# Tree attention on one core: three stores and two layings moved in GpSimd's program, and Q of heads 16 to 31 loaded in rows of sixteen nodes

## The chip, the cores and the metric

The kernel runs on one core of a Trainium2 chip. The core has a matrix engine (TensorE, called PE in the profile, with PEld for its weight loads), a vector engine (VectorE, DVE), a scalar engine (ScalarE, ACT), a general engine (GpSimd, POOL) and sixteen DMA engines that serve queues filled by POOL, SP and ACT. The metric is the device time of one execution in microseconds; the median over several runs is given. Before the change it is 132.79 us (3 runs, 132.54 to 132.94).

## The reference

Attention over 96 heads (8 x 12), each with 512 nodes of width 64, in float32. The nodes are those of a binary tree in heap order, and a node attends only to itself and its ancestors:

```python
mask = np.zeros((seq, seq))
for i in range(seq):
    mask[i, i] = 1
    parent = i
    while parent > 0:
        parent = (parent - 1) // 2
        mask[i, parent] = 1

scores = np.einsum('bhqd,bhkd->bhqk', Q, K) * scale
scores = scores + (1 - mask) * (-1e9)
weights = np.exp(scores - np.max(scores, axis=-1, keepdims=True))
weights = weights / (np.sum(weights, axis=-1, keepdims=True) + 1e-10)
return np.einsum('bhqk,bhkd->bhqd', weights, V).astype(np.float32)
```

Q, K and V have 12.6 MB each, and so has the output.

## The kernel before

**Pairs, quads and blocks.** The kernel works on pairs of heads, 48 of them, numbered i. For each pair it forms scores in two parts (`scores1`: the upper nodes as keys, `scores2`: each query's own tile of leaves), with the mask added as a product of codes on TensorE, takes exponentials on ScalarE (two instructions for the first part's 1024 columns and the second part's halves), multiplies by V with a column of ones (`values`), and divides on VectorE (`norm`: a reciprocal of the column of sums and a product). `head(i, a)` tells which two heads a pair has. Loads come in blocks: K and Q in blocks of 8 heads (`KB`), V in blocks of 16 (`VB`). The block number of V is called o below.

**Three forms of Q and K.** A load casts float32 to bf16 and lays nodes on partitions. In the narrow form (pairs below `WIDE` = 8, heads 0 to 15) a partition holds 4 nodes of one head, in rows of 512 bytes of bf16. In the wide form two heads share the partitions and a row has 8 nodes (1024 bytes); in the far form four heads share them and a row has 16 nodes (2048 bytes). Q is far from pair `FAR` = 16 on (head 32), K from pair `KFAR` = 24 on (head 48). `turn` transposes K or Q of a pair (narrow) or of two pairs (wide and far) on TensorE into `ktp` or `qtp`, and VectorE copies them to where the matmuls read them. The far form of Q is turned in two halves of a quad of pairs; `far_q` hands on the queries of all four pairs (`qTs`) only when its second half has been copied. From pair `FAR` on a pair of a quad has heads 8j + r and 8j + r + 4.

**V.** It lands in a staging tile, `vst`, of which there are three. From block 1 on its rows come in parts: "upper" (the first 64 rows), and "even" and "odd" in block 1 or "leaves0" and "leaves1" in later blocks. Copies (`spread`) bring pieces of it to the places of the matmul operand `vt`, of which there are two, on VectorE (table `BY_VECTOR`, then `STEADY_VECTOR`), on ScalarE (`BY_SCALAR`, `STEADY_SCALAR`) and on GpSimd (`spread_top`, `spread_pool`). `far_codes` are four small copies on ScalarE that lay out the mask's codes for the far form of Q; `FAR_CODES` gives the pairs at which they are done.

**What sets the order.** Nothing is scheduled automatically; every engine works in the order in which the program emits instructions for it. The main loop over i follows a string of steps for each pair: S (both scores of pair i), V (values and norm of pair i - 1), K and Q (the next turn), D and A (the table's V copies on VectorE and ScalarE, at the end if the letter is missing), W (a small copy of codes), X (idle matmuls). `FIRST` holds the strings of the first pairs; later ones repeat with period 2 or 4.

**GpSimd's program.** GpSimd issues almost all DMAs: the loads (`load_k`, `load_q`, `load_v`, `load_rows`) and nearly all stores, each of a block of 8 heads, 1024 KB. It also copies V, and for the last two blocks of K and Q (80 to 87 and 88 to 95) it lays heads side by side in another tile (`lay_beside`). All these are entries of one list, `pool_program()`, taken strictly in order; `ready` tells from which pair on an entry may be emitted. A wait of one entry holds back all after it. Before the change the stores are put into the list by a rule: `BEHIND` = 56 heads behind the loads.

Of the kernel before, what the change touches and what calls it, by code (L numbers as in the profile page):

```python
# [13 lines left out]
BEHIND = 56  # L14
# [105 lines left out]
def kernel(  # L120
# [15 lines left out]
    WIDE, FAR, KFAR = 8, 16, 24  # L136
# [622 lines left out]
    def pool_program():  # L759
# [5 lines left out]
            (load_q, 12, 4), (load_k, 16, 4), (load_rows, 1, "upper"),  # L765
            (load_q, 16, 4), (load_rows, 1, "even"), (load_k, 20, 4), (load_rows, 1, "odd"),
            (load_q, 20, 4), (load_k, 24, 8), (load_q, 24, 4), (load_rows, 2, "upper"),
            (load_q, 28, 4), (load_rows, 2, "leaves0", "leaves1"), (load_k, 32, 8), (load_q, 32, 8),
# [7 lines left out]
        loaded, stored = 72, 0  # L776
        for h in range(56, NH, KB):
            top = [(spread_top, h // VB + 0)] if h % VB == 8 and 4 <= h // VB + 0 < NH // VB else []
            if top:
                top.append((spread_pool, (h // VB, "Z0", 0, 16), (h // VB, "Z1", 0, 16)))  # L780
            ops += [(load_k, h, KB)] + top + [(load_q, h, KB)]
            if h == 64:
                ops.append((
                    spread_pool, *[(3, part, 0, 16) for part in ("Z0", "Z1", "X", "M", "D1")]
                ))
            while loaded < min(h + 32, NH):
                names = ("leaves0", "leaves1") if loaded % VB else ("upper",)
                ops.append((load_rows, loaded // VB) + names)
                loaded += KB
            if top:  # L790
                o = h // VB
                ops.append((spread_pool, *[(o, part, 0, 16) for part in ("X", "M", "D1")]))
            if stored + KB + BEHIND <= h + KB:
                ops.append((store, nc.gpsimd, stored, KB))
                stored += KB
        ops.insert(-1, (lay_beside, "kst", 80 // KB))
        while stored < NH - KB:
            n = 2 if stored == APART else 0
            ops.append((store, nc.gpsimd, stored + n, KB - n))
            if stored == 40:  # L800
                ops.append((lay_beside, "qst", 80 // KB))
            if stored == 64:
                ops += [(lay_beside, "kst", 88 // KB), (lay_beside, "qst", 88 // KB)]
# [169 lines left out]
```

## Time and profile before

| | |
|---|---|
| median of 3 runs | 132.79 us |
| profiled execution | 132.49 us |
| its span, first to last instruction | 130.7 us |
| mean granted clock | 0.986 |
| bytes moved, as the DMA packets count them | 32.25 MB |
| HBM read, written | 37.94 MB, 12.58 MB |

The profile is one execution. A timeline row has the start, the busy time, the engine, the line of the kernel, the operation and its tiles; in brackets stands how long the engine was idle before it and what ended that. A row of the windows table has, after the window, for each engine the busy time and the number of instructions, then the granted clock, the mean share of the DMA engines that packets took (above 1 where an engine has several packets under way) and GB/s. A row of the chain of waits has start, length and what the chain passed through. A row of the DMA issues has the number of DMAs, KB of each and the median time from issue to landing.

### The profile page before, as it was taken

The numbers are of one execution on the slowest core, as the hardware profiler recorded it, in microseconds if no ns is written. First come the engines' busy times: TensorE is split into PE (matmuls) and PEld (weight loads), VectorE is DVE, ScalarE is ACT, GpSimd is POOL, SyncE is SP. The second block draws the span as 40 slices with busy tenths as digits, with TensorE's granted clock in tenths as the row PEclk, the third lists the DMA queues.
The fourth block names the chain that finished last, engine by engine and source line by source line (L and its number), as shares of the span: only waits on it lengthen the run. The fifth ranks groups of instructions, "written<-read, shape, count | busy, mean of one in ns | idle before, by whom it ended". The sixth has DMA issues, their size and how long they took to land.

```text
span 130.7 us, 5436 instructions
## 1 busy us (share of the span) xinstructions
PE 113.7 (87%) x2353; PEld 81.0 (62%) x2353; DVE 105.6 (81%) x254; ACT 101.1 (77%) x163; POOL 84.4 (65%) x116
## 2 busy tenths in 40 slices
PE   6688969999799887899998999896999997999940
PEld 2354755766577566677776786674677675776630
DVE  3349779888999998989998998987898997894560
ACT  4179676989779995968987799797689785889930
POOL 6999625354483999995299899953999963202130
PEclk9999999999999999999999999999999999999995
DMA  2999999999999999999999999999999999999984
GB/s 89 248 190 192 201 195 201 201 202 205 201 203 208 208 205 207 208 210 205 207 211 201 283 292 210 270 309 231 338 228 322 257 277 397 402 404 386 382 339 145
DMA packets 26071, 32.25 MB, mean 247 GB/s; under 512 B 1240, under 2 KB 19544, under 8 KB 26048
## 3 DMA queue, kind: packets, MB, share of 16 engines
q0 software_dynamic: 24384, 30.41, 111.4%
q1 hardware_dynamic: 944, 0.91, 2.2%
q10 hardware_dynamic: 720, 0.59, 1.5%
q8 instruction: 18, 0.29, 0.8%
q14 instruction: 5, 0.04, 0.1%
HBM read 37.94 MB, written 12.58 MB: 386 GB/s over the span
## 4 chain that ended last, share of the span: by engine, by line
DVE 29%; DMA 28%; PE 22%; POOL 7%; ACT 6%; issue 4%; ACTq 0%; DVEq 0%; POOLq 0%
DMA vst<-in_V_dram 17%; DMA qst<-in_Q_dram 11%; DVE of L735 9%; PE ob L696 8%; DVE vt L374 6%; PE s L601 3%; DVE qq L577 3%; ACT e L652 3%; DVE rec L733 3%; DVE kk L521 3%; POOL kst L247 2%; PE s L608 2%; DVE kk L525 2%; POOL qst L247 2%; ACT e L618 2%
## 5 line engine op out<-in xcount | busy, mean ns | idle before, releaser
L618 ACT ACTIVATE e<-s 128x1024 bf16<-128x1024 f32 x40 | 40.9, 1024 | 15.0 <-PE s L608 14.6
L696 PE MATMUL ob<-vt,e 128*128 128x65 bf16 (+1 forms) x940 | 37.1, 197 | 2.6 <-DVE of L735 1.0
L696 PEld LDWEIGHTS <-e 128*128 128x128 bf16 (+1 forms) x960 | 30.1, 102 | 9.6 <-DVE of L735 1.9
L374 POOL COPY vt<-vst 32x512 int32<-32x512 int32 (+4 forms) x44 | 32.5, 739 | 4.7 <-PE ob L696 2.5
L652 ACT ACTIVATE e<-s 128x384 bf16<-128x384 f32 x80 | 34.7, 490 | 0.0
L735 DVE TENSOR_TENSOR of<-ob,rec 128x512 f32<-128x512 f32 x47 | 32.5, 691 | 1.6
L374 DVE COPY vt<-vst 32x1024 bf16<-32x1024 bf16 (+5 forms) x47 | 20.9, 445 | 2.8 <-DMA vst<-in_V_dram 1.9
L743 POOL DMA_DIRECT2D out_dram<-of x13 | 11.5, 888 | 12.9 <-DVE of L735 12.4
L733 DVE RECIPROCAL rec<-ob 128x8 f32<-128x8 f32 x47 | 9.5, 202 | 9.9 <-PE ob L696 9.3
L257 POOL DMA_DIRECT2D kst<-in_K_dram x11 | 8.0, 725 | 7.4 <-DMA qst<-in_Q_dram 3.2
L601 PE MATMUL s<-far,codes 40*128 40x512 bf16 x64 | 12.5, 386 | 0.0
L635 PEld LDWEIGHTS <-codes 40*128 40x128 bf16 x80 | 6.2, 94 | 8.7 <-issue 3.9
L614 ACT ACTIVATE e<-s 128x1024 bf16<-128x1024 f32 x8 | 8.2, 1023 | 4.1 <-PE s L608 4.0
L577 DVE COPY qq<-qtp 128x1024 bf16<-128x1024 bf16 x16 | 10.9, 680 | 0.3 <-PE qtp L572 0.3
L635 PE MATMUL s<-far,codes 40*128 40x384 bf16 x64 | 10.7, 324 | 0.4 <-ACT e L652 0.2
L257 POOL DMA_DIRECT2D qst<-in_Q_dram x12 | 8.5, 708 | 3.8 <-DMA vst<-in_V_dram 1.9
L374 ACT COPY vt<-vst 32x512 int32<-32x512 int32 (+3 forms) x19 | 10.4, 545 | 0.4
L608 PE MATMUL s<-qq,kk 64*128 64x512 bf16 x48 | 9.2, 378 | 1.0 <-DVE qq L577 1.0
L646 PEld LDWEIGHTS <-kk 64*128 64x128 bf16 x192 | 8.4, 94 | 2.6
L521 DVE COPY kk<-ktp 128x256 bf16<-128x256 bf16 x24 | 9.0, 414 | 0.7 <-PE ktp L513 0.7
L302 POOL DMA_DIRECT2D vst<-in_V_dram x7 | 5.6, 800 | 6.0 <-DMA vst<-in_V_dram 4.3
L572 PE MATMUL qtp<-ptile,qst 128*64 128x128 bf16 x192 | 7.5, 221 | 1.7 <-DVE qq L577 1.0
(64 smaller groups left out, 178.2 us busy)
## 6 DMA issues: line engine op xcount, KB each, us to landing
out_dram<-of POOLq DMA_DIRECT2D x10, 1024.0 KB, 15.2
kst<-in_K_dram POOLq DMA_DIRECT2D x9, 512.0 KB, 16.5
qst<-in_Q_dram POOLq DMA_DIRECT2D x8, 512.0 KB, 14.8
vst<-in_V_dram POOLq DMA_DIRECT2D x12, 256.0 KB, 13.5
vst<-in_V_dram POOLq DMA_DIRECT2D x6, 512.0 KB, 12.9
qst<-in_Q_dram POOLq DMA_DIRECT2D x6, 256.0 KB, 12.1
kst<-in_K_dram POOLq DMA_DIRECT2D x4, 256.0 KB, 10.3
out_dram<-of POOLq DMA_DIRECT2D x1, 768.0 KB, 13.0
```

Of the source, the lines that this page charges most:

```text
L257: return nc.gpsimd.dma_start(out=kept[b][:, h0 % KB:h0 % KB + n, :, :].rearrange("p (g x) t d -> p g (x t d)", x=x), in_=src[:, h0 // x:(h ...
L374: return copy(out=dst, in_=src)
L521: nc.vector.tensor_copy(out=columns(flat, 32 * unit, (640, 4), (step, 2), (4, 8), (1, 4)), in_=columns(kp, base, (256, 4), (128, 2), (1, 8 ...
L577: nc.vector.tensor_copy(out=qqs[j][:, :, 8 * last:8 * last + 8, :].rearrange("p b u c -> p b (u c)"), in_=quarters,)
L601: nc.tensor.matmul(out=sp[:, a, :], lhsT=(k1code if i < WIDE else k1wide)[64 * a:64 * a + CODE_ROWS, :], rhs=(q1code, q1wide, q1far)[(i >= ...
L608: nc.tensor.matmul(out=sp[:, a, :], lhsT=keys(i, a, TOP), rhs=qTs[i][64 * a:64 * a + 64, :, :].rearrange("p t c -> p (t c)"), start=False, ...
L618: ) if i < WIDE else nc.scalar.activation(
L635: nc.tensor.matmul(out=flat[:, a, :, :].rearrange("p u (t c) -> p u t c", t=4)[:, :, :, 32 // n:], lhsT=k2wide[64 * a:64 * a + CODE_ROWS, ...
L652: nc.scalar.activation(out=e2s[i % NE][:, a, :, 32:128].rearrange("p t (r u) -> p t r u", u=n), in_=flat[:, a, :, :].rearrange("p u (t r) ...
L696: nc.tensor.matmul(out=ob[lo:hi, a, 65 * t:65 * t + 65], lhsT=e[:, a, PLACE[t], lo:hi], rhs=vt[vtile[tile_v][0]][:, head(i, a) % VB, vtile ...
L733: nc.vector.reciprocal(out=rec[:, a:a + n, :, :], in_=o4[:, a:a + n, :, D:D + 1])
L735: nc.vector.tensor_tensor(out=ofs[j][:, h0:h1 + 1:head(i, 1) - head(i, 0), :, :], in0=o4[:, a:a + n, :, 0:D], in1=rec[:, a:a + n, :, :].to ...
```

## The change

GpSimd's list from head 56 on is written out by hand. Against the old order:

- Store of heads 8 to 15 stands behind the loads of K and Q of heads 72 to 79 and the V copies there; store 16 behind K and Q of 80; store 24, with store 32, behind K and Q of 88, the V copies of block 5 and the laying of block 80. (Store 0 keeps its place behind the leaves of V block 4.)
- The upper rows of V block 5 stand behind K and Q of 64, GpSimd's copies of V block 3 and the leaves of block 5, where they stood ahead of store 0 and of K of 64.
- Both layings of block 80 stand ahead of stores 24 and 32, both of block 88 ahead of stores 40 to 64.

For heads 16 to 31, `FAR` becomes 8: the wide form of Q isn't used any more, pairs 8 to 15 take their heads as quads do, and both halves of Q of a quad are turned before its first scores (steps Q at pairs 6 and 7 for pairs 8 to 11, at 10 and 11 for pairs 12 to 15; before at 6, 8, 10 and 12). K and Q of heads 16 to 31 are loaded eight heads at a time, and "upper", "even" and "odd" of V block 1 stand behind Q of heads 16 to 23. The far codes are laid out at pairs 4 to 7 and ScalarE's three first copies of V block 1 are done at pair 8 together.

```diff
-    WIDE, FAR, KFAR = 8, 16, 24
+    WIDE, FAR, KFAR = 8, 8, 24
...
-            (load_q, 12, 4), (load_k, 16, 4), (load_rows, 1, "upper"),
-            (load_q, 16, 4), (load_rows, 1, "even"), (load_k, 20, 4), (load_rows, 1, "odd"),
-            (load_q, 20, 4), (load_k, 24, 8), (load_q, 24, 4), (load_rows, 2, "upper"),
-            (load_q, 28, 4), (load_rows, 2, "leaves0", "leaves1"), (load_k, 32, 8), (load_q, 32, 8),
+            (load_q, 12, 4), (load_k, 16, 8), (load_q, 16, 8),
+            (load_rows, 1, "upper"), (load_rows, 1, "even"), (load_rows, 1, "odd"),
+            (load_k, 24, 8), (load_q, 24, 8), (load_rows, 2, "upper"),
+            (load_rows, 2, "leaves0", "leaves1"), (load_k, 32, 8), (load_q, 32, 8),
...
-            if stored + KB + BEHIND <= h + KB:
-                ops.append((store, nc.gpsimd, stored, KB))
-                stored += KB
-        ops.insert(-1, (lay_beside, "kst", 80 // KB))
-        while stored < NH - KB:
-            n = 2 if stored == APART else 0
-            ops.append((store, nc.gpsimd, stored + n, KB - n))
-            if stored == 40:
-                ops.append((lay_beside, "qst", 80 // KB))
-            if stored == 64:
-                ops += [(lay_beside, "kst", 88 // KB), (lay_beside, "qst", 88 // KB)]
-            stored += KB
+        def tops(o):
+            return [(spread_top, o), (spread_pool, (o, "Z0", 0, 16), (o, "Z1", 0, 16))]
+
+        def rest(o):
+            return [(spread_pool, (o, "X", 0, 16), (o, "M", 0, 16), (o, "D1", 0, 16))]
+
+        def out(h0, n=KB):
+            return [(store, nc.gpsimd, h0, n)]
+
+        def leaves(o):
+            return [(load_rows, o, "leaves0", "leaves1")]
...
+        ops += k7 + q7 + leaves(4) + out(0)
+        ops += k8 + q8 + [(spread_pool, *[(3, part, 0, 16) for part in ("Z0", "Z1", "X", "M", "D1")])]
+        ops += leaves(5) + [(load_rows, 5, "upper")]
+        ops += k9 + tops(4) + q9 + rest(4) + out(8)
+        ops += k10 + q10 + out(16)
+        ops += k11 + tops(5) + q11 + rest(5)
+        ops += [(lay_beside, "kst", 80 // KB), (lay_beside, "qst", 80 // KB)] + out(24) + out(32)
+        ops += [(lay_beside, "kst", 88 // KB), (lay_beside, "qst", 88 // KB)]
+        for h in range(40, NH - KB, KB):
+            n = 2 if h == APART else 0
+            ops += out(h + n, KB - n)
         ops += [(store, nc.gpsimd, NH - KB + h, 2) for h in (0, 4)]
...
-        6: [(1, 6, 0, 8)],
-        7: [(1, "Z0", 0, 8)],
-        8: [(1, "Z1", 0, 8)],
+        8: [(1, 6, 0, 8), (1, "Z0", 0, 8), (1, "Z1", 0, 8)],
...
-    FAR_CODES = {9: (0, 0), 10: (64, 0), 11: (0, 1), 13: (64, 1)}
+    FAR_CODES = {4: (0, 0), 5: (64, 0), 6: (0, 1), 7: (64, 1)}
...
-    FIRST = ['KSQ', 'SXKQXDVAKQ', 'SVKQ', 'SKQAV', 'KSVXQA', 'SAKQVDW', 'SKDVQ', 'SVD', 'SVDKQX']
+    FIRST = [
+        'KSQ', 'SXKQXDVAKQ', 'SVKQ', 'SKQAV', 'KSVXQA', 'SAKQVDW', 'SKDVQ', 'SVQD', 'SVDKX', 'SVK',
+        'SVQ', 'SVKQ', 'SV',
+    ]
...
-        elif i == FAR - 1:
+        elif i == 2 * WIDE - 1:
             steps = "SQVK"
```

More of the change, by code (lines that the diff above doesn't have):

```diff
@@ L775, in pool_program @@
         ]
[L776 to L792, printed above, removed]
-            if stored + KB + BEHIND <= h + KB:
-                ops.append((store, nc.gpsimd, stored, KB))
-                stored += KB
@@ new lines, in rest, with qk @@
+        def rest(o):
[4 more added lines that the diff above has]
+            return [(load_rows, o, "leaves0", "leaves1")]
+        def qk(h0):
+            return [(load_k, h0, KB)], [(load_q, h0, KB)]
+        k7, q7 = qk(56)
+        k8, q8 = qk(64)
+        k9, q9 = qk(72)
+        k10, q10 = qk(80)
+        k11, q11 = qk(88)
+        ops += k7 + q7 + leaves(4) + out(0)
```

1 line of the change is left out of this document (removed).

## The prediction

> **What bounds the kernel now.** I read the page first (busy shares, the DMA row), then a table by windows, then the timelines of the engines round the places that the change touches.
>
> ```profile
> PE 113.7 (87%) x2353; PEld 81.0 (62%) x2353; DVE 105.6 (81%) x254; ACT 101.1 (77%) x163; POOL 84.4 (65%) x116
> DMA  2999999999999999999999999999999999999984
> 10.00:20.00 10.00, 8.39 (x176) 5.56 (x172) 8.17 (x24) 7.58 (x12) 5.88 (x9) 1.00 1.44 196
> 50.00:60.00 10.00, 9.42 (x229) 7.07 (x224) 8.94 (x21) 6.72 (x12) 9.06 (x16) 1.00 1.19 209
> 110.00:120.00 10.00, 9.76 (x189) 7.15 (x187) 8.02 (x18) 8.46 (x16) 0.83 (x1) 1.00 1.03 400
> 125.00:129.50 4.50, 0.75 (x16) 0.52 (x14) 1.76 (x5) 0.18 (x1) 0.45 (x1) 0.74 0.83 291
> 129.50:130.70 1.20, 0.00 (x0) 0.00 (x0) 0.00 (x0) 0.00 (x0) 0.00 (x0) 0.50 0.00 0
> ```
>
> In the window rows the last three numbers are the granted clock, the DMA share and GB/s. The DMA engines are full from the second slice to the last but one: about 200 GB/s while the loads land as bf16 (196 with 512-byte rows, 209 with the longer ones), 400 while only stores run. All bytes of the kernel pass this stream in the order in which POOL issues them, and neither their number nor their end changes by moving a store. The stream has slack only at its end: from 125.0 to 129.5 it is 0.83 busy against 1.03 in the window of stores, so 4.5 x (1 - 0.83/1.03) = 0.9 us is empty. No order of stores can win more than about that, call it 1.0.
>
> But the engines stand close to the stream (PE 8.4 to 9.8 of 10 us). Where a load lands just as it is wanted, its place in the stream sets the pace:
>
> ```profile
> 80.91 0.64 PE L513 MATMUL ktp<-ptile,kst 128*64 128x128 bf16 x16 [0.23 <-DMA kst<-in_K_dram]
> 83.62 0.64 PE L572 MATMUL qtp<-ptile,qst 128*64 128x128 bf16 x16 [0.45 <-DMA qst<-in_Q_dram]
> 91.38 0.64 PE L513 MATMUL ktp<-ptile,kst 128*64 128x128 bf16 x16 [0.98 <-DMA kst<-in_K_dram]
> 93.87 0.64 PE L572 MATMUL qtp<-ptile,qst 128*64 128x128 bf16 x16 [0.23 <-DMA qst<-in_Q_dram]
> 85.92 0.21 DVE L733 RECIPROCAL rec<-ob 128x8 f32<-128x8 f32 x1 [0.42 <-PE ob L696]
> 92.06 0.75 DVE L521 COPY kk<-ktp 128x256 bf16<-128x256 bf16 x2 [0.68 <-PE ktp L513]
> 79.25 14.58 DMA qst<-in_Q_dram
> ```
>
> These are the K and Q blocks of heads 64 to 79: the transposes start at landing, PE loses 0.23 + 0.45 + 0.98 + 0.23 = 1.9 us, and VectorE, which is nearly as full, loses 0.42 + 0.68 = 1.1 us of it. The last row is of the chain of waits, which goes through such a landing.
>
> **Part 1, the stores.** One store, as POOL issues it, and the laying that now stands ahead:
>
> ```profile
> 72.36 0.91 POOL L743 DMA_DIRECT2D out_dram<-of  x1
> out_dram<-of POOLq DMA_DIRECT2D x10, 1024.0 KB, 15.2
> 90.23 4.87 POOL L374 COPY vt<-vst 32x512 int32<-32x512 int32 x6 [2.49 <-PE ob L696]
> 95.05 0.70 POOL L257 DMA_DIRECT2D qst<-in_Q_dram  x1
> 95.79 2.95 POOL L374 COPY vt<-vst 32x1024 int32<-32x1024 int32 x3
> 98.93 1.04 POOL L448 COPY kst<-kst 128x1024 int32<-128x1024 int32 x1 [0.19 <-DMA kst<-in_K_dram]
> 100.49 0.61 PE L507 MATMUL ktp<-ptile,kst 128*128 128x128 bf16 x8
> ```
>
> 1024 KB at 400 GB/s is 2.6 us of the stream. Store 8 goes behind K and Q of heads 72, store 16 behind K and Q of 80, store 24 behind K and Q of 88; so from head 72 on each K and Q block has one store less ahead of it and lands 2.6 us earlier. The upper part of V block 5 goes from ahead of K of head 64 to behind Q and the leaves; it is 512 KB at 209, about 2.5 us, and gives heads 64 to 71 the same lead. 2.6 us is more than any wait above, so all four vanish. POOL's own work is unchanged in number (0.91 us a store, 1.04 a laying). The stream doesn't run dry: loads wait some 14 us between issue and landing, and moving one store takes 2.6 of that.
>
> What the waits return: between 1.1 us (VectorE's loss) and 1.9 us (PE's). I take 1.1, as VectorE comes next, and so does POOL: from the values of pair 31, which release POOL at 90.23, to the end of the laying of K it takes 4.87 + 0.70 + 2.95 + 1.04 = 9.6 us, to 99.8 without its 0.19 of waiting; PE takes that K at 100.49 today. A gain of over 0.7 us between these points ends in a wait for POOL. As lower end I keep 0.5, if both bite. The layings ahead of stores 24 to 64 delay these by up to 10 us; the stream still has stores 24 and 32 (5.2 us) behind Q of head 88, more than the about 2.2 us for two layings and an issue: nothing.
>
> **Part 2, longer rows and larger loads.** Heads 16 to 31 of Q, 1 MB as bf16, go from 1024 to 2048 bytes a row. At the worst rate above, 196, they take 5.35 us, at 209 5.0: the stream wins 0 to 0.35 us. I take 0.15, and count it as nothing, since the end follows the last values. Three loads fewer: 3 x 0.7 us of POOL (the row at 95.05), which isn't the bound there. The Trainium skill, "DMA: Bandwidth & Descriptors", section "Anatomy of one DMA", has a fixed cost of about 2 us for each DMA, besides its bytes; by that, three DMAs fewer would take an estimated 6 us off a queue that ran one at a time. The DMA share of 1.19 to 1.44 in the rows above says that they overlap, and disagrees for this queue.
>
> **Part 3, the front.** Here Q's new form costs: in quads of pairs, both halves of Q must be turned and copied before the quad's first scores.
>
> ```profile
> 18.50 12.18 DMA vst<-in_V_dram
> 25.45 1.02 ACT L614 ACTIVATE e<-s 128x1024 bf16<-128x1024 f32 x1
> 30.75 1.35 DVE L374 COPY vt<-vst 128x1024 bf16<-128x1024 bf16 x3 [0.44 <-DMA vst<-in_V_dram]
> 32.08 0.62 ACT L374 COPY vt<-vst 32x512 int32<-32x512 int32 x1
> 33.09 1.02 DVE L374 COPY vt<-vst 32x1024 bf16<-32x1024 bf16 x3
> 35.14 0.68 DVE L549 COPY qq<-qtp 128x1024 bf16<-128x1024 bf16 x1
> 35.17 0.67 ACT L396 COPY far<-codes 40x512 bf16<-40x512 bf16 x1
> 42.28 0.90 DVE L374 COPY vt<-vst 32x1024 bf16<-32x1024 bf16 x2
> 43.20 0.21 DVE L733 RECIPROCAL rec<-ob 128x8 f32<-128x8 f32 x1
> 44.05 0.68 DVE L549 COPY qq<-qtp 128x1024 bf16<-128x1024 bf16 x1
> 51.68 0.38 PE L608 MATMUL s<-qq,kq 64*128 64x512 bf16 x2
> 52.16 1.02 ACT L618 ACTIVATE e<-s 128x1024 bf16<-128x1024 f32 x1 [1.56 <-PE s L608]
> 52.35 0.79 PE L696 MATMUL ob<-vt,e 128*128 128x65 bf16 x20
> 53.08 0.87 ACT L652 ACTIVATE e<-s 128x384 bf16<-128x384 f32 x2
> ```
>
> VectorE's work there is the same, in another order, so I book what it waits.
> - The "odd" rows of V block 1 land at 18.50 + 12.18 = 30.7, and VectorE waits for them. They now stand behind 256 KB more of Q: 0 to 1.3 us at 200 GB/s, since both loads are in the stream together today. I take +0.55. That wait then covers the copy of Q's second half (0.68, at 35.14 today), due at pair 7 now: -0.7.
> - The code copies (L396, 0.67) go from pairs 9, 10, 11, 13 to 4 to 7; at 4 and 5 nothing leaves in exchange, so the exponentials from 25.45 on come up to 1.3 us later. On VectorE most of it falls into the wait at 30.75: 0.1 (0 to 0.6). After pair 9 ScalarE gets the time back.
> - At pair 8 ScalarE copies three pieces of V in one go, and values(8) need them all. Q's copy ends at 31.3, the exponential starts 0.5 later (51.68 to 52.16), two exponentials 1.8, three pieces 1.9, values 0.8: 36.3. VectorE has the first norm at 32.8 (31.3 and 1.5 through scores and values, 51.68 to 53.14), 0.85 for it (43.20 to 44.05), 1.0 of V, 1.0 of K (34.11 to 35.14): 35.7. It waits 0.6 at most; with copies that overlap a little, 0.4 (0 to 1.0).
> - At pair 12 the scores wait for Q's copy, which VectorE now does behind norm(10) and K; today it runs after norm(11), at 44.05. From there to the end of the values is 1.5 us again, and VectorE has only the 0.90 of row 42.28 meanwhile: it idles 0.6. For norm(12), the exponentials of 12 end 2.3 after the key matmuls (51.68 to 53.95), the second scores of 13 need the buffer then freed (0.4, from 51.68 to 52.35 less the 0.3 that the key matmuls take), the values take 0.79: 3.5. VectorE has by then done 1.5, a norm of 0.85 and a piece of V of 0.45 to 0.9: about 3.0, so 0.5 more. Together 1.1 (0.5 to 2.0; the upper end if ScalarE's 1.56 at 52.16 is lost whole once more).
>
> Sum of the front: 0.55 - 0.7 + 0.1 + 0.4 + 1.1 = +1.45, call it 1.5, with ends 0.5 and 2.5. No load is late between there and 80.91, so nothing gives it back before the waits above.
>
> **POOL in the middle.** The first copies of V block 3 overwrite rows that belong to heads 24 to 27; in the new order of heads these are read up to pair 15, not 13.
>
> ```profile
> 48.65 5.35 POOL L374 COPY vt<-vst 32x1024 int32<-32x1024 int32 x7
> 53.95 0.84 POOL L302 DMA_DIRECT2D vst<-in_V_dram  x1
> 62.88 0.70 POOL L257 DMA_DIRECT2D kst<-in_K_dram  x1 [1.81 <-DMA qst<-in_Q_dram]
> 65.43 0.70 POOL L257 DMA_DIRECT2D qst<-in_Q_dram  x1 [1.85 <-DMA vst<-in_V_dram]
> ```
>
> Values of pair 15 end at 53.14 + 1.5 = 54.6; the last four of the seven copies end at 53.95 today and could only start then, so what is queued behind them (V upper of block 4, K, Q and leaves) is issued some 2.7 us later. POOL waits 1.81 + 1.85 = 3.7 us for landings soon after, which swallows it, and the stream holds 14 us: nothing (0 to 0.5).
>
> **The sum.** +1.5 (front) - 1.1 (waits returned) = +0.4 us at the last values, and the end follows them. The profiled execution is 132.49 us, 130.7 of span and 1.8 around it: 132.9. The median of the runs shown, 132.79, is 0.3 above; on it the forecast is **133.2 us**. With the ends (0.5 to 2.5, less 1.9 to 0.5) it is -1.4 to +2.0, and the stream stops the gain at -1.0: 131.8 to 134.8.
>
> **Rivals.**
> 1. *The earlier loads win* (faster). Price 1.9 us at 80.91 to 93.87, all on PE's path, against a front of 0.5 to 0.9. It decides where the front costs less than what the waits return. For it speaks that PE, not VectorE, is named in all four rows; against it POOL's 9.6 us and that VectorE is 0.9 full in the front. Bounded by the stream: -1.0, 131.8; its middle 132.1. Chance 0.24.
> 2. *It cancels out*, or the end of the stream holds the time: within 0.3, 132.8. For it speaks the full DMA row. Chance 0.14.
> 3. *POOL turns into the bound.* Its late copies at 54.6 aren't swallowed, or the laying of K at 99.8 makes PE wait although the loads are there: the waits return 0.5 or less and the front costs 2: +1.5, 134.3. Chance 0.14.
> 4. *Fewer, larger transfers shorten the stream*: the 1 MB of Q and as much of its neighbours gain all of 196 to 209, 2 x 0.35 = 0.7 at most, middle 0.5: 132.3. The page of the Trainium skill named above points that way with its fixed cost. The rows show a stream that is full without it. Chance 0.03.
>
> **How the numbers follow.** The forecast's own case has 0.45 (132.8 to 133.9): 0.31 of it lies above 133.2, 0.14 below. A measurement here tells about 0.3%, 0.4 us, from no change. Slower: 0.31 + 0.14 = 0.45. Faster: rival 1 with 0.22 and rival 4 with 0.03, 0.25. Same: 0.14 + 0.14 + 0.02 = 0.30. The range 131.8 to 134.5 reaches from the stream's floor to past rival 3.
>
> **What would show it.** Transposes of K and Q of heads 64 to 79 without a DMA as releaser; scores of pair 12 released by VectorE's copy, with ScalarE idle some 2 us ahead of them; the values of pair 15 (52.35) 1 to 2 us later; the laying of K right ahead of its transposes; DMA share over 1.0 until about 120. Wrong it is if these values come at the same time, or if K and Q of heads 64 to 79 are still waited for.

## The result and the profile after

The changed kernel takes 136.17 us (median of 6 runs, 135.21 to 136.82), the kernel before 132.77 us beside it (6 runs, 132.53 to 132.94): 1.0247 times as long, 95% interval 1.0216 to 1.0278. It is slower by 3.4 us, where 0.4 was forecast, and lies outside the range of 131.8 to 134.5. A ratio below leaves out runs over 1.5% longer than the fastest of the same kernel, so it can disagree with a median; where many runs are long, as in e2 and e3, both are needed.

The profiled execution took 136.02 us, with a span of 134.3 us against 130.7. From its page: the busy times, the slices of the granted clock and of the DMA engines, and the issues of whole stores.

```profile
PE 115.0 (86%) x2350; PEld 81.8 (61%) x2353; DVE 108.9 (81%) x254; ACT 100.8 (75%) x163; POOL 82.3 (61%) x113
PEclk9999999999999769999999999999999999999995
DMA  3999999999999999999999999999999899999974
out_dram<-of POOLq DMA_DIRECT2D x10, 1024.0 KB, 11.2
```

There are four things to see. The clock has a dip at slices 14 and 15. The DMA engines, which were full to the last slice but one, have a thin slice at 105 us and a thin end. A store now waits 11.2 us from issue to landing and not 15.2: less is queued ahead of it. VectorE has 3.3 us more of work than before (108.9 against 105.6) with the same 254 instructions.

What the forecast had said of the loads came true. The timeline of PE in the changed kernel at K and Q of heads 64 to 79:

```profile
84.13 0.61 PE L512 MATMUL ktp<-ptile,kst 128*64 128x128 bf16 x16
86.20 0.61 PE L571 MATMUL qtp<-ptile,qst 128*64 128x128 bf16 x16
93.57 0.61 PE L512 MATMUL ktp<-ptile,kst 128*64 128x128 bf16 x16
95.64 0.61 PE L571 MATMUL qtp<-ptile,qst 128*64 128x128 bf16 x16
```

None of them has a bracket any more: PE waits for none of these loads.

The last values end later by 2.7 us. VectorE's division for the last pair, 47, is done head by head; it starts at 125.79 us before and here, in the changed kernel's timeline, at 128.47:

```profile
128.47 0.18 DVE L732 RECIPROCAL rec<-s 128x4 f32<-128x4 f32 x1
```

The rest of the 3.5 us of span, some 0.85 us, arises behind the last values. The windows of the kernel before:

```profile
100.00:105.00 5.00, 4.97 (x105) 3.70 (x102) 4.42 (x11) 4.19 (x8) 5.00 (x6) 1.00 1.10 282
105.00:110.00 5.00, 4.31 (x84) 3.15 (x81) 4.35 (x9) 3.50 (x7) 2.62 (x3) 1.00 1.08 338
110.00:115.00 5.00, 5.00 (x104) 3.92 (x102) 4.01 (x10) 4.28 (x9) 0.83 (x1) 1.00 1.02 398
```

and of the changed one, with two short windows in it:

```profile
100.00:105.00 5.00, 4.72 (x101) 3.33 (x97) 4.87 (x11) 4.07 (x8) 4.82 (x6) 1.00 1.08 213
105.00:110.00 5.00, 4.49 (x91) 3.33 (x87) 4.82 (x11) 3.81 (x7) 4.96 (x7) 1.00 0.94 347
110.00:115.00 5.00, 4.54 (x99) 3.49 (x96) 4.05 (x10) 3.62 (x8) 2.39 (x3) 1.00 0.98 330
104.50:106.00 1.50, 1.50 (x38) 1.22 (x33) 1.49 (x4) 1.50 (x3) 1.50 (x3) 1.00 0.75 176
110.50:112.00 1.50, 1.12 (x19) 0.66 (x15) 1.47 (x4) 0.57 (x3) 1.13 (x2) 1.00 0.92 240
```

The last two numbers of a row are the DMA share and GB/s. Before, the share is 1.02 or more in these rows; after, it is 0.94 and 0.98 in the last two windows of 5 us: the stream runs thin at 104.5 to 106 us and again at 110.5 to 112. GpSimd's timeline in the changed kernel says why:

```profile
93.55 4.87 POOL L373 COPY vt<-vst 32x512 int32<-32x512 int32 x6 [6.58 <-issue]
98.37 0.70 POOL L256 DMA_DIRECT2D qst<-in_Q_dram  x1
99.12 2.80 POOL L373 COPY vt<-vst 32x1024 int32<-32x1024 int32 x3
101.98 1.03 POOL L447 COPY kst<-kst 128x1024 int32<-128x1024 int32 x1
102.96 1.23 POOL L447 COPY qst<-qst 128x1024 int32<-128x1024 int32 x1
104.14 1.81 POOL L742 DMA_DIRECT2D out_dram<-of  x2
108.11 3.51 POOL L742 DMA_DIRECT2D out_dram<-of  x4
```

Stores 24 and 32, whose data had been ready since pair 20, are issued from 104.1 us on, behind nine copies and two layings. Between 86.25 and 104.14 us GpSimd issues a single transfer, Q of head 88.

How late each stage is can be read from the starts of VectorE's reciprocals, pair by pair, against the kernel before (us; one profiled execution each; the runs in the other columns follow below):

| norm of pair | changed | late list only | front only | changed, warm | stores first | late list, stores first | mended front |
|---|---|---|---|---|---|---|---|
| | | e1 | e2 | e4 | e9 | e11 | e15 |
| 10 | +0.82 | -0.12 | +1.24 | +0.97 | +1.20 | -0.09 | +1.12 |
| 12 | +2.90 | -0.30 | +2.55 | +2.35 | +2.51 | -0.05 | +2.59 |
| 18 | +2.55 | -0.62 | +2.02 | +1.82 | +1.99 | -0.03 | +2.17 |
| 20 | +3.44 | -0.23 | +2.34 | +2.71 | +2.90 | -0.03 | +3.03 |
| 28 | +3.85 | +0.07 | +2.53 | +3.11 | +3.33 | +0.20 | +3.44 |
| 32 | +2.23 | -1.51 | +0.92 | +1.49 | +1.73 | -1.36 | +1.84 |
| 36 | +2.89 | -0.86 | +1.48 | +2.16 | +3.17 | +0.07 | +2.32 |
| 47 | +2.68 | -1.33 | +1.02 | +1.83 | +2.70 | -0.39 | +1.85 |
| span | +3.53 | +0.64 | +0.98 | +2.58 | +2.67 | +0.22 | +1.82 |

One profile can be off by more than a microsecond. The traces of e1, e8, e11 and e14, which have the old front, lie within 0.25 us of the kernel before at norm 10; that of e10, which has it too, is 1.49 us late there: PE stands still for 1.59 us from 18.86 us on, and the clock falls to 0.50 at 20.40. Differences of a few tenths between single columns say little.

### The profile page after: what moved, and what is told of

Same layout as the page of the kernel before. It is cut to its first block, busy times and chain, and to the rows that moved or that the text cites. A ratio compares the mean times of both kernels' runs of the same rounds, so it can differ in the third digit from the quotient of the medians.

```text
span 134.3 us, 5429 instructions
## 1 busy us (share of the span) xinstructions
PE 115.0 (86%) x2350; PEld 81.8 (61%) x2353; DVE 108.9 (81%) x254; ACT 100.8 (75%) x163; POOL 82.3 (61%) x113
## 4 chain that ended last, share of the span: by engine, by line
DVE 43%; PE 23%; DMA 17%; POOL 5%; ACT 4%; issue 3%; ACTq 0%; POOLq 0%
DVE of L734 14%; DMA vst<-in_V_dram 12%; PE ob L695 9%; DVE vt L373 8%; DMA qst<-in_Q_dram 5%; DVE qq L576 5%; DVE kk L520 5%; DVE kk L524 4%; DVE rec L732 4%; PE s L600 3%; PE s L607 3%; ACT e L617 3%; POOL kst L246 2%; ACT e L651 2%; PE s L634 2%
## 5 line engine op out<-in xcount | busy, mean ns | idle before, releaser
L695 PE MATMUL ob<-vt,e 128*128 128x65 bf16 (+1 forms) x940 | 37.6, 198 | 3.7 <-DVE of L734 2.2
L373 DVE COPY vt<-vst 32x1024 bf16<-32x1024 bf16 (+5 forms) x47 | 24.3, 516 | 3.0 <-DMA vst<-in_V_dram 2.0
L742 POOL DMA_DIRECT2D out_dram<-of x13 | 11.2, 863 | 13.3 <-DVE of L734 13.3
L600 PE MATMUL s<-far,codes 40*128 40x512 bf16 x80 | 15.6, 387 | 0.4 <-PE ktp L472 0.3
L634 PE MATMUL s<-far,codes 40*128 40x384 bf16 x80 | 13.5, 328 | 0.4 <-ACT e L651 0.2
L576 DVE COPY qq<-qtp 128x1024 bf16<-128x1024 bf16 x20 | 13.6, 682 | 0.3 <-PE qtp L571 0.3
L256 POOL DMA_DIRECT2D kst<-in_K_dram x10 | 7.4, 741 | 7.0 <-DMA vst<-in_V_dram 2.6
L571 PE MATMUL qtp<-ptile,qst 128*64 128x128 bf16 x256 | 9.9, 220 | 0.3 <-DVE qq L576 0.3
L645 PE MATMUL s<-qq,kk 64*128 64x160 bf16 (+1 forms) x192 | 8.9, 208 | 0.0
L292 POOL DMA_DIRECT2D vst<-in_V_dram x8 | 5.1, 636 | 6.0 <-DMA vst<-in_V_dram 2.5
## 6 DMA issues: line engine op xcount, KB each, us to landing
out_dram<-of POOLq DMA_DIRECT2D x10, 1024.0 KB, 11.2
kst<-in_K_dram POOLq DMA_DIRECT2D x10, 512.0 KB, 15.2
```

Of the source, the lines that this page charges most:

```text
L373: return copy(out=dst, in_=src)
L576: nc.vector.tensor_copy(out=qqs[j][:, :, 8 * last:8 * last + 8, :].rearrange("p b u c -> p b (u c)"), in_=quarters,)
L600: nc.tensor.matmul(out=sp[:, a, :], lhsT=(k1code if i < WIDE else k1wide)[64 * a:64 * a + CODE_ROWS, :], rhs=(q1code, q1wide, q1far)[(i >= ...
L634: nc.tensor.matmul(out=flat[:, a, :, :].rearrange("p u (t c) -> p u t c", t=4)[:, :, :, 32 // n:], lhsT=k2wide[64 * a:64 * a + CODE_ROWS, ...
L645: nc.tensor.matmul(out=flat[:, a, :, lo:hi], lhsT=keys(i, a, WTILE2[t]), rhs=qT[64 * a:64 * a + 64, :, lo:hi], start=False, stop=t == 1, s ...
L695: nc.tensor.matmul(out=ob[lo:hi, a, 65 * t:65 * t + 65], lhsT=e[:, a, PLACE[t], lo:hi], rhs=vt[vtile[tile_v][0]][:, head(i, a) % VB, vtile ...
```

## The experiments

"Late list" is GpSimd's list from head 56 on, "front" everything else in the change. No run leaves out a part of the computation. Theory F of the first four expectations puts the loss into the front alone; e1 speaks against that.

**e1_late: the late list alone.** The kernel before with the new list from head 56 on.

```diff
-        for h in range(56, NH, KB):
...
+        ops += k7 + q7 + leaves(4) + out(0)
...   (the new list; WIDE, FAR, KFAR = 8, 16, 24, FIRST and the other tables as before)
```

> Only the late part of the change: GpSimd's list from head 56 on as in the changed kernel, the front as before (Q far from pair 16, loads in fours). Theory F (the loss arises in the front: scores of pair 12 wait for Q's copy, PE stands still, then runs at half clock for 3.4 us): the late part costs nothing and returns up to the 1.1 us of load waits: 131.8 to 133.0 us. Theory L (the late part costs: GpSimd's V copies and layings now meet VectorE's V copies, 24.3 us of them against 20.9): 134.0 to 135.5 us, V copies of VectorE near 24 us.

Measured: 133.37 us against 132.67, 1.006 (1.0036 to 1.0084). The values come early as foreseen, 1.33 us at the last pair, and the time is still longer. GpSimd's timeline shows the order at work:

```profile
104.07 1.28 POOL L448 COPY kst<-kst 128x1024 int32<-128x1024 int32 x1 [1.87 <-DMA kst<-in_K_dram]
106.52 1.04 POOL L448 COPY qst<-qst 128x1024 int32<-128x1024 int32 x1 [1.17 <-DMA qst<-in_Q_dram]
107.51 4.34 POOL L743 DMA_DIRECT2D out_dram<-of  x5
```

Five stores that were ready go out at 107.5 us, behind layings that wait for landings. In the kernel before, five of the six stores from 24 to 64 had been issued by 104 us, and the sixth at 104.7. The last packet of the stream lands at 129.7 us, against 129.4 in the kernel before: the end doesn't follow the last values down.

**e2_front: the front alone.** The changed kernel with the old late list.

```diff
-        ops += k7 + q7 + leaves(4) + out(0)
...
+        for h in range(56, NH, KB):
...   (the old rule, with BEHIND = 56; the front as changed)
```

> Only the front of the change: Q of heads 16 to 31 in rows of sixteen, loads in eights, code copies and steps as in the changed kernel; GpSimd's list from head 56 on by the rule of before. Theory F: pair 16 is 2.6 us late as in the changed kernel; the loads of heads 64 to 79 hide part of it: 134.5 to 136.5 us. Theory L: 133.0 to 134.0 us.

Measured: 1.0071 (1.0024 to 1.0118); of seven runs three took 133.0 to 133.5 us and four 134.9 to 135.5. The median, 134.92 us, is 1.7% above the kernel before. By the ratios each half costs some 0.6 or 0.7% and both together 2.5%; by e2's median the front alone costs most of it. So it isn't shown that the two halves cost more together than the sum of each. The three short runs had a mean granted clock of 0.990 to 0.994, three of the four long ones 0.974 to 0.977, the fourth 0.994. The profiled run, of 133.48 us, shows something else: it too is 1.6 us less late at norm 32 than at norm 28, with the old list. Its transposes of K and Q of heads 64 to 79, in PE's timeline:

```profile
83.07 0.61 PE L513 MATMUL ktp<-ptile,kst 128*64 128x128 bf16 x16
85.14 0.61 PE L572 MATMUL qtp<-ptile,qst 128*64 128x128 bf16 x16
92.25 0.61 PE L513 MATMUL ktp<-ptile,kst 128*64 128x128 bf16 x16
```

No wait either: a front that is 2.5 us late finds the loads landed. The waits that the late list was to remove are gone without it. e1, with the old front, gets back 1.58 us by the late list: either half alone removes these waits.

**e3_sqvk and e4_warm: the standstill at pair 12.** e3 turns Q's second half ahead of the values of pair 10, e4 puts six idle matmuls ahead of the scores of pair 12.

```diff
-        'SVQ', 'SVKQ', 'SV',
+        'SVQ', 'SQVK', 'SV',        (e3)
+        'SVQ', 'SVKQ', 'XXXSV',     (e4)
```

> The changed kernel, but at pair 11 the turn of Q stands ahead of the values and of the turn of K (steps S Q V K in place of S V K Q), so VectorE copies Q for pair 12 before norm(10) and the K copies. Theory F: the scores of pair 12 start about 1.7 us earlier, the clock stays full, pair 16 comes 1.5 to 2 us earlier: 134.0 to 135.0 us. Theory L: pair 16 comes earlier, but the end moves by less than 0.7: 135.5 to 136.2 us.

> The changed kernel, with six idle matmuls ahead of the scores of pair 12, in the 1.7 us in which PE stands still there. The wait itself stays. Theory F: if standing still is what halves the clock, no clock below 1.0 between 45 and 50 us, and the about 1 us that norm(12) was later than worked out comes back: 135.0 to 135.6 us. If the clock falls for another reason, it falls again and the time is that of the changed kernel, 136.2.

Measured: e3 1.0137 (1.0113 to 1.016), with a median of 135.77 us in five runs from 134.31 to 137.87; e4 1.0223 (1.0172 to 1.0273). The engines' timeline in the changed kernel at pair 12:

```profile
43.74 0.39 PE L607 MATMUL s<-qq,kq 64*128 64x512 bf16 x2 [1.73 <-DVE qq L576]
44.23 1.02 ACT L617 ACTIVATE e<-s 128x1024 bf16<-128x1024 f32 x1 [2.67 <-PE s L607]
45.26 0.21 DVE L732 RECIPROCAL rec<-ob 128x8 f32<-128x8 f32 x1 [0.30 <-PE ob L695]
46.88 1.20 PE L695 MATMUL ob<-vt,e 128*128 128x65 bf16 x20
47.89 1.05 PE L472 MATMUL ktp<-ptile,kst 128*64 128x128 bf16 x16
48.13 0.21 DVE L732 RECIPROCAL rec<-ob 128x8 f32<-128x8 f32 x1 [1.30 <-PE ob L695]
```

and two windows there, one with the standstill and the one behind it, with the granted clock as the third number from the right:

```profile
42.18:45.59 3.41, 1.76 (x36) 1.37 (x36) 3.03 (x8) 1.36 (x3) 3.18 (x6) 1.00 1.17 208
45.59:49.00 3.41, 3.41 (x52) 2.46 (x50) 2.08 (x5) 2.83 (x6) 3.32 (x4) 0.50 1.37 205
```

The scores wait 1.73 us for Q's copy, ScalarE stands 2.67 us, and then the clock is granted at 0.50 for 3.41 us: values take 1.20 us, transposes 1.05, at a full clock 0.79 and 0.61. In e4 the clock stays at 1. Its window at that place:

```profile
43.90:47.30 3.40, 3.16 (x64) 2.31 (x63) 2.49 (x5) 2.81 (x5) 3.22 (x5) 1.00 1.28 199
```

and the same two steps in its timeline:

```profile
46.75 0.79 PE L695 MATMUL ob<-vt,e 128*128 128x65 bf16 x20
47.37 0.61 PE L472 MATMUL ktp<-ptile,kst 128*64 128x128 bf16 x16
```

Pair 12 adds 1.4 us (+0.97 to +2.35) instead of 2.1 (+0.82 to +2.90). So the half clock costs 0.7 us there; in the times of e4 that is within the interval. That the idle matmuls kept the clock up isn't shown by e4 alone: e2 and e9 have none, and in their profiles PE stands still for 1.62 and 1.63 us there, the clock stays at 1, and pair 12 adds 1.31 us. In those of e5 and e6 it stands still for 1.62 us, and the clock falls as in the change. The last section has what differs.

The whole standstill may be worth more: e3's ratio lies 1.1% or 1.5 us below that of the change. But two of its five runs, 136.6 and 137.87 us, are as long as the change's longest or longer, and in its profile, of the run of 136.6 us, pair 12 adds only 0.43 us and the clock falls all the same, at 47.94 us.

**e5_refill and e8_refill_late: two stores moved ahead of the layings.** The same edit on the changed kernel (e5) and on e1 (e8).

```diff
-        ops += k11 + tops(5) + q11 + rest(5)
-        ops += [(lay_beside, "kst", 80 // KB), (lay_beside, "qst", 80 // KB)] + out(24) + out(32)
+        ops += k11 + out(24) + tops(5) + q11 + out(32) + rest(5)
+        ops += [(lay_beside, "kst", 80 // KB), (lay_beside, "qst", 80 // KB)]
```

> The changed kernel with two stores moved in POOL's program: store 24 right behind K of head 88 (ahead of the top copies of block 5), store 32 behind Q of head 88 (ahead of the rest of block 5); everything else as changed. Theory S (the DMA stream runs dry behind the layings and that sets the end): between 100 and 115 us the stream is full again (it loses 0.3 us or less instead of 1.6), and the time falls by 0.8 to 1.6 us from 136.2: to 134.6 to 135.4. At most 0.9 us of it can show, if the last values still come at about 128.5 us, because the 4.9 us from there to the end stay (norm 47 at 125.8 us in a span of 130.7 before). Theory C (only the late compute counts, the gaps in the stream are harmless): 136.0 to 136.5. A third: Q of head 88 comes 1 to 3 us later behind the moved stores and its laying with it, so that PE waits for it: 136.8 to 138.

> The kernel before with the late list of the change (as measured: 133.4 us) and the same move of stores 24 and 32 ahead of the copies of block 5. Theory S: with the early front the stream loses only 0.15 us (at 108.5 to 109.5 us), so the move is worth 0 to 0.3 us: 133.0 to 133.4; the stream's last packet stays at 129.4 to 129.7 us although the last values come 1.3 us earlier than in the kernel before. If the layings ahead of the stores were the cost of the late list, the time falls below the kernel before: 131.5 to 132.5.

Measured: e5 135.49 us, 1.0199 (1.017 to 1.0228), e8 134.86 us, 1.0152 (1.0108 to 1.0197). e5 gains 0.7 us; e8, which was to gain 0 to 0.3, loses 1.5. e8's timeline of GpSimd:

```profile
103.71 1.28 POOL L448 COPY kst<-kst 128x1024 int32<-128x1024 int32 x1 [3.14 <-DMA kst<-in_K_dram]
108.66 1.04 POOL L448 COPY qst<-qst 128x1024 int32<-128x1024 int32 x1 [3.66 <-PE ob L696]
109.64 3.53 POOL L743 DMA_DIRECT2D out_dram<-of  x4
```

and two of its windows:

```profile
108.00:109.50 1.50, 1.50 (x34) 1.20 (x30) 0.82 (x3) 1.25 (x3) 0.84 (x1) 1.00 0.85 323
109.50:111.00 1.50, 1.50 (x40) 1.29 (x36) 1.47 (x6) 1.31 (x3) 1.50 (x3) 1.00 0.59 225
```

Q of head 88 now stands behind store 24 in the stream and lands at 108.5 us. Its laying waits for that, four stores wait behind the laying, and nothing else is queued: the stream falls to 0.59. (The row names PE as the releaser; the landing at 108.54 us is 0.1 us ahead of the laying.) The hole had only moved.

**e9_between, e10_late_between and e11_late_both: no ready store behind a laying that waits.** On e5 (e9), on e1 (e10) and on e8 (e11):

```diff
-        ops += [(lay_beside, "kst", 88 // KB), (lay_beside, "qst", 88 // KB)]
-        for h in range(40, NH - KB, KB):
+        ops += out(40) + out(48) + [(lay_beside, "kst", 88 // KB)] + out(56) + out(64)
+        ops += [(lay_beside, "qst", 88 // KB)]
+        for h in range(72, NH - KB, KB):
```

> The changed kernel with no laying ahead of a store that could go first: store 24 ahead of the top copies of block 5, store 32 behind Q of head 88, stores 40 and 48 ahead of the laying of K of head 88, 56 and 64 ahead of that of Q. Theory L (a laying waits for its load to land, every store behind it is issued only then, and the queue of transfers has run empty): the stream is full from 100 to 120 us (380 GB/s or more between 110 and 120, where moving stores 24 and 32 alone left 299 in the first half), and the stream's end goes back to what the last values ask for: 1.0 to 1.6 us less than 136.2, 134.6 to 135.2, or 0.3 to 0.9 us less than the 135.5 with the stores 24 and 32 alone. Theory C (the late values alone set the end): as measured there, 135.3 to 135.7.

> The kernel before with the late list of the change and one edit: stores 40 and 48 ahead of the laying of K of head 88, stores 56 and 64 ahead of that of Q; stores 24 and 32 stay behind the layings of head 80 as in the change. Theory L: the last thin stretch of the stream (0.15 us at 108.5 to 109.5 us, and stores issued at 107.5 us and later) goes, compute still ends 1.3 us earlier than in the kernel before, and the stores of the end no longer queue behind stores 40 to 80: 132.2 to 133.0. If the stream of bytes itself has a floor at the last packet of the kernel before (129.4 us): 132.6 to 133.2.

> The same with stores 24 and 32 moved ahead as well (24 ahead of the top copies of block 5, 32 behind Q of head 88): the run with that move alone took 134.9 us, because the laying of Q of head 88 waited for a load that stood behind the two stores, and stores 40 and on behind the laying were issued at 109.6 us with the queue empty. Theory L: with 40 to 64 ahead of the layings that hole (2 us at 108 to 111) is closed, and the time falls by 1.8 to 2.5 us to 132.3 to 133.1. If the time stays at 134 or above, the hole was not the cause.

Measured: e9 135.20 us, 1.0177 (1.0146 to 1.0207); e10 133.09, 1.0013 (0.9993 to 1.0033); e11 132.95, 1.0007 (0.9986 to 1.0028). From e8 to e11 it is 1.9 us, by that one edit, and e11's window where the hole was reads

```profile
108.00:111.00 3.00, 2.77 (x52) 2.00 (x51) 2.05 (x6) 1.87 (x5) 1.04 (x1) 1.00 1.03 400
```

So layings ahead of stores cost 0.4 us by the medians (0.7 by the ratios) with the early front (e1 to e11). With the late one the change to e9 gains 1.0 us, but the stream isn't all that differs there. PE stands still as long in e9's profile (1.63 us) as in e5's (1.62); behind it the clock falls in e5 and not in e9, as their windows show:

```profile
41.42:44.84 3.42, 1.80 (x43) 1.22 (x38) 3.34 (x8) 0.86 (x3) 2.35 (x5) 1.00 1.20 214
44.84:48.25 3.41, 3.41 (x54) 2.45 (x51) 2.06 (x4) 3.36 (x7) 3.27 (x5) 0.50 1.35 199
39.76:43.17 3.41, 2.72 (x68) 2.03 (x65) 3.28 (x9) 1.99 (x4) 1.78 (x4) 1.00 1.24 211
43.17:46.58 3.41, 2.22 (x38) 1.50 (x39) 2.94 (x7) 1.95 (x4) 3.23 (x5) 1.00 1.20 202
```

The first two rows are e5's, the others e9's. With the clock halved in both profiles, the change to e5 gains 0.7 us. The trace says 0.85: in e5 and e9 the span is as much longer (3.19 and 2.67) as the last values are late (3.21 and 2.70), and what the change lost behind them is gone.

**e6_mid, e7_all and e12_front_all: the middle.** e6 issues K and Q of head 56 ahead of GpSimd's copies of block 3, which wait 4.17 us for the values of pair 15. e7 is e6 with e5's edit and the idle matmuls, e12 is e7 with the edit of e9.

```diff
-            ... (2, "D1", 0, 16)), (spread_top, 3, 0, 12),
+            ... (2, "D1", 0, 16)),
+            (load_k, 56, 8), (load_q, 56, 8), (spread_top, 3, 0, 12),
...
-        ops += k7 + q7 + leaves(4) + out(0)
+        ops += leaves(4) + out(0)
```

> The changed kernel with K and Q of head 56 issued ahead of POOL's top copies of block 3 instead of behind them; these copies wait 4.2 us for the values of pair 15. Theory S: K of head 56 is issued at about 53 us instead of 60, the stream is full between 60 and 70 us (about 205 GB/s instead of 187 and 197), all later loads land 0.5 to 0.8 us earlier, and the time falls by 0 to 0.8 us: 135.4 to 136.2. Theory C: 136.0 to 136.5, since no transposition of heads 56 to 79 waits for its load. A rival: the earlier reservation of the buffers makes POOL wait for the transposes of head 24, and the top copies come later: 136.5 to 137.

> The changed kernel with the two edits before (stores 24 and 32 ahead of the copies of block 5, K and Q of head 56 ahead of those of block 3) and with the six idle matmuls ahead of the scores of pair 12 that kept the clock at 1. If the three causes (half clock, dry stream in the middle, dry stream behind the layings) are the whole of what the front and the late list cost together beyond each alone, the time is that of a front 1.0 to 1.8 us late with a full stream: 133.5 to 134.5. If it stays at 135 or above, something else binds (VectorE's slower copies of V, for one).

> The changed kernel with everything found mended but the later front itself: stores ahead of the layings, K and Q of head 56 ahead of the copies of block 3, six idle matmuls ahead of the scores of pair 12. Theory: what is left is the front's own lateness, 1.0 to 1.8 us at the last values: 133.7 to 134.5 (135.07 without the stores ahead of the layings). If it comes to 132.8 or less, the front costs nothing by itself; at 135 or above, the stream was not it.

Measured: e6 1.0221 (1.0169 to 1.0273), an interval too wide to tell it from the change; e7 135.07 us, 1.0153 (1.0121 to 1.0186), and e12 135.22 us, 1.0169 (1.0135 to 1.0202), where 133.5 to 134.5 and 133.7 to 134.5 were expected. With the stream mended and a full clock in its profile e12 is still 1.7% slower, so a part of the cause was missing.

**e13_front_warm, e14_lay_first and e15_front_lay_first: the rest.** e12's transposes of head 80 wait for GpSimd; PE's timeline in e12:

```profile
103.36 0.62 PE L506 MATMUL ktp<-ptile,kst 128*128 128x128 bf16 x8 [0.99 <-POOL kst L447]
```

A store ahead of that laying delays it by 0.9 us, so e14 (on e11) and e15 (on e12) put the laying first. e13 is e2 with e4's idle matmuls.

```diff
-        ops += k11 + out(24) + tops(5) + q11 + out(32) + rest(5)
-        ops += [(lay_beside, "kst", 80 // KB), (lay_beside, "qst", 80 // KB)]
+        ops += k11 + out(24) + tops(5) + q11 + rest(5)
+        ops += [(lay_beside, "kst", 80 // KB)] + out(32) + [(lay_beside, "qst", 80 // KB)]
```

> The kernel before with only the front of the change, as measured before (133.0 to 133.5 us in three of its runs, 134.9 to 135.5 in four), and with six idle matmuls ahead of the scores of pair 12, which compute nothing that is used. If the half clock behind PE's standstill at pair 12 is what parts the two groups, it does not come any more and all runs lie at 132.9 to 133.7. If the two groups stay, something else parts them, and the clock costs only the 0.7 to 0.9 us that the changed kernel showed.

> The kernel before with the late list of the change, mended: store 24 ahead of the top copies of block 5, the laying of K of head 80 at once behind the rest of block 5 (so PE does not wait 1.0 us for it at pair 36, as it did with store 32 ahead of it), then store 32, the laying of Q of head 80, stores 40 and 48, the laying of K of head 88, stores 56 and 64, the laying of Q. Theory: the last values come 1.0 to 1.4 us earlier than in the kernel before and the stream stays full; if the end follows the values down, 131.6 to 132.3; if the bytes still to be moved set it (the kernel before lost only some 0.8 us of its stream behind 120 us), 132.2 to 132.8.

> The changed kernel with everything mended (K and Q of head 56 ahead of the copies of block 3, six idle matmuls ahead of the scores of pair 12, store 24 ahead of the copies of block 5) and the laying of K of head 80 ahead of store 32. Theory P (POOL's chain from the values of pair 31 to this laying makes PE wait at pair 36): norm 36 comes 0.7 to 1.2 us earlier than with store 32 ahead of the laying, and the time is 134.0 to 134.6 instead of 135.2. If it stays at 135, the lateness at pairs 20 and 36 has another cause.

Measured: e13 133.68 us against 133.06, 1.0057 (1.0024 to 1.0091), with one of its eleven runs, of 329.5 us, far off the others; e14 133.03 us, 1.000 (0.9976 to 1.0025); e15 134.43 us, 1.017 (1.0096 to 1.0244). e15's last values are late by 1.85 us and not 2.49 as in e12, and the wait of 0.99 us is gone; the interval of its time is too wide to show that, since three runs took 134.3 to 134.4 us and two 136.1 to 136.2. The two long ones had a mean granted clock of 0.972 and 0.975, the others 0.985 to 0.993. e13's ten other runs no longer fall into two groups, but reach from 133.0 to 135.6 us with clocks of 0.985 to 0.996, so the half clock isn't all that parts the runs of the front. e14 equals the kernel before: even in the best order found, the late list is worth nothing, and no run beat both kernels.

## Why the prediction was wrong

The forecast had +0.4 us at the last values and an end that follows them. Measured were 2.68 and, behind them, 0.85. Three steps carry the miss: pair 12, mis-sized by 1.0 us, the middle, put at nothing and 1.3 us in the trace, and the stream, which did run dry. By the steps of the prediction:

- **"The layings ahead of stores 24 to 64 ... nothing" and "the stream doesn't run dry"** failed. The working counted bytes behind Q of head 88, but stores 24 and 32 were themselves behind the layings, and the layings behind a chain that the late front had made later: the copies ahead of them start at 93.55 us instead of 90.23. The 2.2 us for two layings and an issue are also a slip, as the prediction's own rows give 2 x 1.04 + 0.91 = 3.0. Cost: 0.85 us in the trace, 0.7 us by e5.
- **"The end follows" the last values** failed. e1 has them 1.33 us earlier and takes 0.7 us longer; e14 with a full stream has 0.51 us and no gain. The prediction had seen the limit, 0.9 us of empty stream at the end, but used it only to bound a gain.
- **The waits returned, -1.1**, were right in place and larger in size: -1.62 us between norms 28 and 32, where VectorE's V copies also take 0.39 us less (1.38 instead of 1.77). But they can be returned only once, and the front's lateness does it already: with the old list the front gets back 1.61 us (e2). Beside that front the late list's own share of the sum was nothing.
- **"At pair 12 ... 1.1 (0.5 to 2.0)"**: mis-sized. The waits are those worked out: scores 1.73 us behind Q's copy, VectorE 0.30 us ahead of norm 11 and 1.30 ahead of norm 12 (forecast 0.6 and 0.5). It took 2.08 us, 1.4 in e4 and 1.31 in e2 and e9 without the half clock, which the prediction didn't have and which came in some profiles only.
- **The front up to pair 10**, +0.35 us as 0.55 - 0.7 + 0.1 + 0.4, measured +0.82, and +0.97 to +1.24 in the other columns with this front. By pair 18, 0.35 us of what pair 12 had cost were returned, which wasn't foreseen.
- **"POOL in the middle ... nothing (0 to 0.5)"** failed: 1.30 us from norm 18 to 28, 0.89 of it at pair 20. The late issue did no harm by itself; e12 issues these loads early and has the same step (+1.77 to +2.70 us). What goes with it is that GpSimd's copies now run beside VectorE's copies of V, and these became slower. The page's groups have them, before

```profile
L374 DVE COPY vt<-vst 32x1024 bf16<-32x1024 bf16 (+5 forms) x47 | 20.9, 445 | 2.8 <-DMA vst<-in_V_dram 1.9
```

and after

```profile
L373 DVE COPY vt<-vst 32x1024 bf16<-32x1024 bf16 (+5 forms) x47 | 24.3, 516 | 3.0 <-DMA vst<-in_V_dram 2.0
```

The 3.4 us between 20.9 and 24.3 are all that VectorE's busy time has grown by. Two of the 47 are those between the norms of pairs 18 and 20, in VectorE's timeline of the kernel before

```profile
62.26 0.42 DVE L374 COPY vt<-vst 32x1024 bf16<-32x1024 bf16 x1
64.78 0.42 DVE L374 COPY vt<-vst 32x1024 bf16<-32x1024 bf16 x1
```

and in VectorE's and GpSimd's of the changed one:

```profile
64.81 0.47 DVE L373 COPY vt<-vst 32x1024 bf16<-32x1024 bf16 x1
65.09 4.46 POOL L373 COPY vt<-vst 32x1024 int32<-32x1024 int32 x4
67.39 1.25 DVE L373 COPY vt<-vst 32x1024 bf16<-32x1024 bf16 x1
```

The copy that runs beside GpSimd's four takes 1.25 us, the one ahead of them 0.47. Together they are 0.89 us longer, which is the step of 0.89 us at pair 20. The other profiles agree: between norms 18 and 20 V copies and lateness grow by 0.33 and 0.32 us in e2, by 0.91 and 0.91 in e9, by 1.04 and 1.04 in e13, and by nothing in e11. So the slower copies are the step at pair 20. That GpSimd's copies slow them is read from the overlap; no run moved these away. From norm 20 to 28 V copies take 1.01 us more and the lateness grows by 0.41, which isn't taken apart.

- **From norm 32 to the end** +0.45 us came that the prediction didn't have. The laying of K of head 80 ends at 103.0 us and its transposes start at 103.07, as foreseen.
- **Longer rows, nothing,** stands: between 20 and 35 us the stream moves 208, 199 and 208 GB/s in windows of 5 us, against 200, 202 and 205 before, which is 1% or 0.2 us, and the end doesn't follow it. The estimate of 6 us by the Trainium skill's fixed cost for each DMA found no support.

The sum of these lags, of one profile, is 0.82 + 2.08 - 0.35 + 1.30 - 1.62 + 0.45 = 2.68 us. Rival 3, in which GpSimd becomes the bound, came nearest with 134.3, in part by luck: GpSimd's late work in the middle does cost, but PE doesn't wait for the laying of head 80 in the change, and the rival left out the transfers that GpSimd issues too late and VectorE's slower copies. The prediction's own upper end, 134.8, was cut to 134.5 without a reason; the result lies above both. What stays open: why the mended front (e15) is 1.85 us late at the last values where the same front with the old list was 1.02 in one profile and 1.95 in another (e13), what else than the clock scatters the runs with this front, and why e4 gains less in time than in its trace.

## What to carry to other kernels

An instruction that waits for a landing should not stand ahead of transfers that are ready in the same in-order list: the queue empties while it waits, and the loss is that of the stream, not of the instruction. Before crediting removed waits to one part of a change, ask whether another part that makes the consumer later removes them too; they can be returned only once. And where the stream of bytes is nearly full to its end (here some 0.9 us of it was empty), earlier values are worth nothing (e1, e11, e14), while a thin stream or later values cost time (e8, e9).

## What the runs showed of the hardware

- A standstill of PE of 1.73 us, with 1.76 us of work in the 3.41 us ahead, was followed by 3.41 us at a clock of 0.50. The Trainium skill, "TensorE: Matmul & The Clock Gate", section "What's actually happening" of Part 1, gives a free-running window of 3413 ns and half the clock after an idle one; the length agrees. Its advice to avoid gaps above some 3 us ("Why this matters for your kernels") wasn't enough here: with half of the window ahead idle the clock fell. Standstills of 1.62 us in e2's profile and 1.63 in e9's were not punished, one of 1.62 in e5's was, which fits a window that runs free.
- The seven stretches of 3.41 us at half clock in the middle of the 17 profiles (the change, e3, e5, e6, e10) each begin a whole number of steps of 3.41 us ahead of the half clock that ends their trace: 45.59 us in the change is 25 steps of 3.414 us ahead of 130.93. The steps just ahead of the seven held 1.70 to 2.00 us of PE work; the other steps from 6 us on, without the last of each trace, held 2.04 us or more. In e9 such a step ends at 43.17 us, inside the standstill, so that the steps on both sides keep 2.2 us of work or more, while in e5 the whole standstill lies in one step, which has 1.80. So whether a standstill of this length is punished depends on where it falls. That one kernel's executions differ by this fits the mean granted clock of the change's six runs (0.983 and 0.984 in the two shortest, 0.972 to 0.975 in the others), but there are no two traces of one kernel to show it. At the very end the clock also fell behind steps with up to 2.28 us (e3), so 2.0 us is no rule for that place.
- Two copies on VectorE took 1.16 and 1.25 us beside copies on GpSimd, and the median of all is 0.42 us. Not every copy beside GpSimd's is slower: in the kernel before one at 75.58 us took 0.43. The Trainium skill, "SBUF — State Buffer", section "Who interferes with whom", says that the two engines share a pair of ports as an exclusive lock. The trace fits: the 0.83 us on top of 0.42 are less than one of GpSimd's copies beside it, 4.46 / 4 = 1.1 us.
- With one load of 512 KB left in the queue, issued 6 us earlier, and two stores only just being issued behind it, the stream fell to a share of 0.75 at 176 GB/s (104.5 to 106 us in the changed kernel). One transfer alone may not fill the sixteen engines; no run tried it apart.
